# Conditioning matmuls of the second layer, moved from the first MLP to three stage changes

## The chip, the cores and the metric

The kernel runs on one core of a Trainium2 chip. The metric is the device time of one execution in microseconds (us). The kernel before took 1434.49 us (median of 3 runs, 1434.38 to 1434.61). The profile is one further execution with the hardware profiler on.

In the profile PE is the matrix engine (TensorE), PEld its weight load, DVE is VectorE, ACT is ScalarE, POOL is GpSimd, SP is SyncE, which issues DMAs here. L119 is line 119 of the kernel's file.

## What is computed

One inference step of a two-layer decoder trunk with width 1024: 512 prompt tokens and 8 samples of 4 tokens, 544 columns in all. Each layer has a token mixer and a squared-ReLU MLP, and every sub-layer is wrapped in normalisation and in shift, scale and gate vectors that come from a conditioning vector.

```python
def ada_params(c, w, b):
    mod = jax.nn.silu(c) @ w + b
    return jnp.split(mod[:, None, :], 6, axis=-1)
...
    for layer in range(DEPTH):
        sh_m, sc_m, g_m, sh_f, sc_f, g_f = ada_params(c, ada_w[layer], ada_b[layer])
        hin = rmsnorm(x, norm_g[layer, 0]) * (1.0 + sc_m) + sh_m
        j = layer // N_MIXERS
        if layer % N_MIXERS == 0:
            mix, buf, hn = rglru_mixer(hin, ...)
        else:
            mix, v = chunk_sgu_mixer(hin, ...)
        x = x + g_m * rmsnorm(mix, norm_g[layer, 1])
        hf = rmsnorm(x, norm_g[layer, 2]) * (1.0 + sc_f) + sh_f
        f = jnp.square(jax.nn.relu(hf @ mlp_w_up[layer])) @ mlp_w_down[layer]
        x = x + g_f * rmsnorm(f, norm_g[layer, 3])
```

`ada_w` is 1024 x 6144 per layer (24 MB). Each of its six sections of 1024 columns makes one vector per sequence, nine sequences in all. Section 0 (shift) and 1 (scale) of layer 1 are first needed when the first MLP ends, section 2 (gate), 3 and 4 when the gating unit ends, section 5 when the second MLP ends.

## The kernel before

Everything runs with features on the partitions and tokens on the free axis; the 544 tokens are two halves of 272 columns. A large product is done as three matmuls on split operands (high x high, high x low, low x high), issued by `mm3` through `mm`; both end in line 119, 128 x 128 weights against 272 columns, so nearly all matmuls carry the line L119. The names say what they multiply: HH and HL are the split normalised input, hi and lo the split weights, hh and hl the split hidden activations of the MLP, yh and yl those of a mixer's output.

The program's order is written by a counter of large matmuls (`Clock`, one tick per `mm`). Side work is a generator; `yield 44` means that its next piece is issued 44 large matmuls later. A scheduler then sets each engine's final order within what the data allow, so what was issued together may be parted.

The stages follow each other: RG-LRU mixer, first MLP, gating unit, second MLP. Each ends in `final_proj`, which projects first half 0, then half 1 of the tokens. After each half a `Stat` sums squares (ACT and DVE) and takes the mean over the features by one matmul with `dmean` (L390). A `Chain` per half then scales, adds the residual (L662), takes a second `Stat` and writes HH (ACT, L452) and HL (DVE, L453) for the next stage. That next stage starts in `first_sweeps`, half 0 first, one k-tile of HH after the other. So half 1 of the old projection covers the chain of half 0, and the sweep over half 0 covers the chain of half 1.

The conditioning of layer 1 is made by `ada_gen`, added as a task of the first MLP: three blocks of 2048 columns, each in eight steps of one k-tile. A step is two loads of 512 KB from SP's queue into the weight pool and four matmuls (L609) with a stationary operand of 32 columns, `tile_position=(0, 32 * g)`, so that the four use four column groups of PE. After eight steps a block is copied, turned by four transposes (L620) and added to the bias (`ada_add`, L568). `every` is 85 ticks.

The gating unit's `vsmp` has two more users of the narrow mode: L1397, in fours, and L1403, one alone with 256 columns.

Of the kernel before, what the change touches and what calls it, by code (L numbers as in the profile page):

```python
# [12 lines left out]
ALU = mybir.AluOpType  # L13
PSUM = bass.MemoryType.PSUM

P = 128
# [64 lines left out]
def trunk_kernel(  # L81
# [511 lines left out]
    def ada_gen(jobs, every):  # L593
        def load(l, blk, k):
            ts_ = [wtile("ada") for _ in range(2)]
            for i in range(2):
                c = blk * 2048 + i * 1024
                nc.sync.dma_start(ts_[i], ada_w[l, k * P:(k + 1) * P, c:c + 1024])
            return ts_

        steps = [(l, b, k) for l, b in jobs for k in range(KD)]
        nxt = load(*steps[0])
        yield every
        for i, (l, blk, k) in enumerate(steps):
            ts_, nxt = nxt, load(*steps[i + 1]) if i + 1 < len(steps) else None
            if k == 0:
                ps = aux()
            for g in range(4):
                nc.tensor.matmul(  # L609
                    ps[32 * g:32 * g + 32, :], scT[:, k, :], ts_[g // 2][:, (g % 2) * 512:(g % 2) * 512 + 512],  # L610
                    start=(k == 0), stop=(k == KD - 1), tile_position=(0, 32 * g))
            if k < KD - 1:
                yield every
                continue
            raw = slot("adas")
            A.copy(raw[:, 0:512], ps)
            yield 12
            pt = aux()
            for q in range(4):
                nc.tensor.transpose(pt[:, q * P:(q + 1) * P], raw[:, q * P:(q + 1) * P], ident)  # L620
            ptv = pt.rearrange("p (q g s) -> p q g s", q=4, g=4)
            for g in range(4):
                c = blk * 2048 + g * 512
                ada_add(l, c // D, (c % D) // P, 4, ptv[:, :, g, 0:9])
            for idx in ((0,), (1,), (2, 3))[blk]:
                ada_derive(l, idx)
            yield every - 12

    class Chain:


# [55 lines left out]
    def first_sweeps(key, chains, evac):  # L687

        for h in range(2):
            for grp in ((0, 1, 2, 3), (4, 5)):  # L690
                lhs = [st.get(key(m // 2)).lhs(m % 2) for m in grp]
                ps = [acc() for _ in range(len(grp) // 2)]
                for k in range(KD):
                    chains[h].need(k)
                    for i in range(len(grp)):
                        for a in (0, 1):
                            mm(ps[i // 2][:, i % 2, 0:HW], lhs[i][k][a], HH[:, k, HS[h]], k + a == 0, False)
                for i, m in enumerate(grp):
                    for k in range(KD):
                        mm(ps[i // 2][:, i % 2, 0:HW], lhs[i][k][0], HL[:, k, HS[h]], False, k == KD - 1)  # L700
                    if i % 2:
                        for j in range(2):
                            evac(m - 1 + j, ps[i // 2][:, j, 0:HW], h)

    def mix_add(m, ps, first):
# [3 lines left out]
        else:  # L709
            V.tensor_tensor(mv, mv, ps[:, :, 0:HW], op=ALU.add)  # L710

    def final_proj(lhs, rhs, both, groups, l, idx, nxt):


        A.activation(warm, epsc, AF.Abs_reciprocal_sqrt)
        S = [Stat(), Stat(nxt is None)]
        rows = LastRows(AM[l][idx]) if nxt is None else None
        for m in both:
            ps = acc()
            mm3(ps, lhs(m), rhs, (0, 1))  # L720
            mix_add(m, ps, False)
            for h in range(2):
                S[h].add(MIX[:, m, HS[h]])
        if rows:
            rows.add(both)
        chains = []
        for h in range(2):
            for grp, parts in groups[h]:
                if rows and h == 1 and grp[-1] == KD - 1:
                    rows.residual()  # L730
                if rows and h == 1 and grp[-1] == KD - 1:
                    for j, m in enumerate(grp):
                        ps = acc()
                        mm3(ps, lhs(m), rhs, (1,), col=0)
                        V.tensor_tensor(MIX[:, m, HS[1]], MIX[:, m, HS[1]], ps[:, 0, 0:HW], op=ALU.add)
                        S[1].add(MIX[:, m, HS[1]])
                        rows.finish_tile(j)
                    break
                ps = [acc() for _ in range(len(grp) // 2)]
                for ks in parts:  # L740
                    for i, m in enumerate(grp):
                        mm3(ps[i // 2], lhs(m), rhs, (h,), ks=ks, col=i % 2)
                        if i % 2 and ks is parts[-1]:
                            mv = MIX[:, m - 1:m + 1, HS[h]]
                            V.tensor_tensor(mv, mv, ps[i // 2][:, :, 0:HW], op=ALU.add)
                            S[h].add2(mv, slot("sq")[:, 0:T].rearrange("p (j n) -> p j n", j=2))
                            if rows and h == 1:
                                rows.add((m - 1, m))
            if rows and h == 1:
                rows.finish(S[1])  # L750
            else:
                chains.append(Chain(l, idx, S[h], h, nxt))
        return chains
# [475 lines left out]
    def state_out():  # L1229
        for (src, n, outs) in ((HST, 9, ((0, 1, h_prompt.rearrange("l s d -> (l s) d")),  # L1230
                                         (1, 9, h_sample.rearrange("l s d -> (l s) d")))),
                               (CST, 27, ((0, 3, conv_prompt.rearrange("l s j d -> (l s j) d")),
                                          (3, 27, conv_sample.rearrange("l s j d -> (l s j) d"))))):
            for b in range(3):
                pt = aux()
                for q in range(4):
                    nc.tensor.transpose(pt[0:n, q * P:(q + 1) * P], src[:, 4 * b + q, :], ident)
                o = slot("st")
                V.tensor_copy(o[0:n, 0:512], pt[0:n, :])
                for lo_, hi_, dst in outs:  # L1240
                    nc.gpsimd.dma_start(dst[:, b * 512:(b + 1) * 512], o[lo_:hi_, 0:512])
                yield 30
# [8 lines left out]
    def mlp(l, nxt, chains, tasks):  # L1251
        for q in range(4):
            hh, hl = [None] * 8, [None] * 8

            def evac(m, ps, h=None):
                if hh[m] is None:
                    hl[m] = slot("hl", F32R)
                    hh[m] = slot("hh", F32R)
                w = slot("hf")
                if h is None:  # L1260
                    dl, dh, dw = [t_[:, 0:T].rearrange("p (h n) -> p h n", h=2) for t_ in (hl[m], hh[m], w)]
                else:
                    dl, dh, dw = hl[m][:, HS[h]], hh[m][:, HS[h]], w[:, HS[h]]
                A.activation(dw, ps, AF.Relu)  # L1264
                A.activation(dw, dw, AF.Square)
                A.copy(dh, dw)  # L1266
                V.tensor_tensor(dl, dw, f32(dh), op=ALU.subtract)  # L1267

            if q == 0:
                first_sweeps(lambda c: ("u", l, 0, c), chains, evac)  # L1270
                for t in tasks:
                    clk.add(t)
            for c in range(3 if q == 0 else 0, 4):
                u = st.get(("u", l, q, c))
                for j in range(2):
                    ps = acc()
                    mm3(ps, u.lhs(j), hin_rhs, (0, 1))
                    evac(2 * c + j, ps[:, :, 0:HW])
            rhs = list(zip(hh, hl))
            if q == 3:  # L1280
                return final_proj(lambda m: st.get(("d", l, 3, m // 2)).lhs(m % 2), rhs, (0, 1),
                                  (singles(range(2, 8), 8),) * 2, l, 3, nxt)
            for c in range(4):
                u = st.get(("d", l, q, c))
                for j in range(2):
                    ps = acc()
                    mm3(ps, u.lhs(j), rhs, (0, 1))
                    mix_add(2 * c + j, ps, q == 0)
# [79 lines left out]
    def spatial_gate(chains):  # L1368
# [40 lines left out]
            V.bn_stats(stat[0:NSMP, 4, c, :], v)  # L1409

        first_sweeps(lambda c: ("su", c), chains, u_evac)
        t_prep = clk.add(sg_prepare(), 10)
        vts = []
        for c in range(6):
# [139 lines left out]
                nc.sync.dma_start(y_prompt[0, c0:c1, b * 512:(b + 1) * 512], o[0:n, 0:512])  # L1554
                yield 6

    chains = mlp(0, (1, 0), chains, [ada_gen([(1, 0), (1, 1), (1, 2)], 85), state_out()])
    chains = spatial_gate(chains)
    chains = mlp(1, None, chains, [])
    clk.drain(*[t for t in clk.tasks])  # L1560
# [30 lines left out]
```

## Time and profile before

| | |
|---|---|
| median of 3 runs | 1434.49 us |
| the profiled execution | 1435.27 us |
| its span on the core | 1433.5 us |
| PE busy | 1395.7 us (97%) |
| VectorE, ScalarE, GpSimd busy | 703.7, 632.5, 41.1 us |
| chain that ended last | PE 65%, of it L119 58% and L609 3%; issue 26% |
| mean granted clock of PE | 0.989 |
| bytes moved | 165.71 MB, 116 GB/s mean |

The span runs from the first to the last instruction. Busy time of PE is modelled, since matmuls overlap each other. A wait in a timeline stands in brackets, with what ended it. The chain of waits is followed back from the last instruction; "issue" in it is time in which the engine waited for nothing that the profile shows. A matmul on 32-bit operands that are not split is two instructions on PE, so a step of four L609 matmuls reads x8.

### The profile page before, as it was taken

How to read it: one execution, taken by the hardware profiler on the slowest of the kernel's cores; microseconds unless marked ns; L12 is line 12 of the kernel's file. 1: busy time of each engine (PE TensorE's matmuls, PEld its weight loads, DVE VectorE, ACT ScalarE, POOL GpSimd, SP SyncE). 2: the span in 40 equal slices, each digit the busy share in tenths (PEclk: the TensorE clock that was granted, in tenths of full speed). 3: DMA queues.
4: the chain of work that ended last, by engine and by line, in shares of the span. 5: the costliest groups of instructions: out<-in, count | busy, mean ns of one | idle time of the engine just before them, and what ended most of it. 6: DMA issues, size and time to landing. Idle time of an engine off the chain costs nothing.

```text
span 1433.5 us, 27033 instructions
## 1 busy us (share of the span) xinstructions
PE 1395.7 (97%) x11472; PEld 1319.4 (92%) x11472; DVE 703.7 (49%) x1442; ACT 632.5 (44%) x1160; POOL 41.1 (3%) x76
## 2 busy tenths in 40 slices
PE   8999999998999999999998999999899999999997
PEld 6899989997999999999997989999899999999996
DVE  4767476779422332333349446653972233333334
ACT  4465746846523413414425434432573341432523
POOL 1200000000100000000000200000000000000000
PEclk8999999999999999999999999999999999999998
DMA  9554554321545545543221333122232222222201
GB/s 309 174 173 130 163 151 149 103 89 60 180 154 174 170 157 173 170 157 115 62 86 60 95 96 107 61 74 62 90 100 91 89 89 89 89 89 89 89 1 63
DMA packets 132227, 165.71 MB, mean 116 GB/s; under 512 B 10168, under 2 KB 111560, under 8 KB 132106
## 3 DMA queue, kind: packets, MB, share of 16 engines
q1 hardware_dynamic: 130346, 161.89, 35.9%
q0 software_dynamic: 1760, 2.09, 0.7%
q8 instruction: 90, 1.47, 0.4%
q14 instruction: 31, 0.25, 0.1%
HBM read 161.31 MB, written 2.65 MB: 114 GB/s over the span
## 4 chain that ended last, share of the span: by engine, by line
PE 65%; issue 26%; DVE 5%; ACT 2%; DMA 1%; POOL 0%; SPq 0%; POOLq 0%; ACTq 0%; DVEq 0%
PE acc L119 58%; PE aux L609 3%; DVE lo L182 1%; PE acc L1478 1%; DVE MIX L448 1%; DVE X L662 1%; DMA xsr<-in_x_sample_dram 1%; DVE HL L453 1%; PE aux L1397 0%; PE aux L580 0%; DVE MIX L660 0%; PE aux L390 0%; ACT HH L452 0%; DVE rs L414 0%; DVE R L415 0%
## 5 line engine op out<-in xcount | busy, mean ns | idle before, releaser
L119 PE MATMUL acc<-HH,hi 128*128 128x272 f32 x1776 | 399.2, 293 | 12.6 <-ACT HH L452 11.2
L119 PE MATMUL acc<-HH,lo 128*128 128x272 f32 x1776 | 394.0, 292 | 3.4 <-DVE lo L182 3.4
L182 DVE TENSOR_TENSOR lo<-raw,hi 128x512 fp32r<-128x512 f32 (+1 forms) x404 | 263.2, 682 | 254.3 <-ACT hi L181 188.1
L119 PE MATMUL acc<-HL,hi 128*128 128x272 f32 x1776 | 355.4, 289 | 3.5 <-DVE HL L453 3.1
L181 ACT CAST hi<-raw 128x512 fp32r<-128x512 f32 (+1 forms) x404 | 230.3, 613 | 281.7 <-PE acc L119 159.2
L119 PEld LDWEIGHTS acc<-HH,hi 128*128 128x128 f32 x1776 | 293.6, 191 | 23.2 <-ACT HH L452 13.7
L119 PEld LDWEIGHTS acc<-HH,lo 128*128 128x128 f32 x1776 | 293.1, 191 | 11.5 <-issue 6.7
L119 PEld LDWEIGHTS acc<-HL,hi 128*128 128x128 f32 x1776 | 273.5, 189 | 10.9 <-issue 5.4
L119 PE MATMUL acc<-hh,lo 128*128 128x272 f32 x1024 | 230.0, 290 | 0.0
L119 PE MATMUL acc<-hh,hi 128*128 128x272 f32 x1024 | 229.8, 290 | 0.0
L119 PE MATMUL acc<-hl,hi 128*128 128x272 f32 x1024 | 229.7, 290 | 0.0
L119 PEld LDWEIGHTS acc<-hh,hi 128*128 128x128 f32 x1024 | 168.0, 188 | 3.9 <-issue 3.8
L119 PEld LDWEIGHTS acc<-hh,lo 128*128 128x128 f32 x1024 | 168.1, 188 | 3.7 <-issue 3.6
L119 PEld LDWEIGHTS acc<-hl,hi 128*128 128x128 f32 x1024 | 168.1, 188 | 3.6 <-issue 3.5
L1267 DVE TENSOR_TENSOR hl<-hf,hh 128x544 fp32r<-128x544 f32 (+1 forms) x76 | 47.7, 634 | 175.2 <-ACT hh L1266 175.0
L1264 ACT ACTIVATE hf<-acc 128x544 f32<-128x544 f32 (+1 forms) x76 | 41.2, 550 | 128.1 <-PE acc L119 126.1
L710 DVE TENSOR_TENSOR MIX<-MIX,acc 128x544 f32<-128x544 f32 x44 | 31.6, 717 | 75.9 <-PE acc L119 75.9
L119 PE MATMUL acc<-hi,HH 128*128 128x256 f32 x192 | 54.8, 285 | 0.0
L119 PE MATMUL acc<-hi,HL 128*128 128x256 f32 x192 | 54.6, 284 | 0.0
L119 PE MATMUL acc<-lo,HH 128*128 128x256 f32 x192 | 53.8, 280 | 0.0
L119 PE MATMUL acc<-yh,hi 128*128 128x272 f32 x208 | 52.7, 291 | 0.3 <-ACT MIX L708 0.3
L119 PE MATMUL acc<-yh,lo 128*128 128x272 f32 x208 | 52.6, 291 | 0.0
(332 smaller groups left out, 1444.5 us busy)
## 6 DMA issues: line engine op xcount, KB each, us to landing
ada<-in_ada_w_dram SPq DMA_DIRECT2D x96, 512.0 KB, 4.9
raw<-in_mlp_w_up_dram SPq DMA_DIRECT2D x64, 512.0 KB, 4.3
raw<-in_mlp_w_down_dram SPq DMA_DIRECT2D x64, 512.0 KB, 4.5
raw<-in_lru_w_in_dram SPq DMA_DIRECT2D x24, 512.0 KB, 4.5
raw<-in_sg_w_in_dram SPq DMA_DIRECT2D x24, 512.0 KB, 4.6
raw<-in_sg_w_out_dram SPq DMA_DIRECT2D x12, 512.0 KB, 4.2
raw<-in_lru_w_out_dram SPq DMA_DIRECT2D x8, 384.0 KB, 3.0
raw<-in_lru_w_out_dram SPq DMA_DIRECT2D x6, 512.0 KB, 6.4
```

Source lines behind the costliest of these rows:

```text
L119: nc.tensor.matmul(out, lhsT, rhs, start=start, stop=stop)
L181: A.copy(h_, raw[:, c:c + st])
L182: V.tensor_tensor(l_, raw[:, c:c + st], f32(h_), op=ALU.subtract)
L448: V.scalar_tensor_tensor(wv, X[:, k, c0:c1], Am[:, k, 0:1], R[:, c0:c1], op0=ALU.mult, op1=ALU.mult)
L453: V.scalar_tensor_tensor(HL[:, k, c0:c1], wv, sh[:, k, 0:1], f32(HH[:, k, c0:c1]), op0=ALU.add, op1=ALU.subtract)
L609: nc.tensor.matmul(ps[32 * g:32 * g + 32, :], scT[:, k, :], ts_[g // 2][:, (g % 2) * 512:(g % 2) * 512 + 512], start=(k == 0), stop=(k == ...
L662: V.scalar_tensor_tensor(X[:, j, c0:c1], MIX[:, j, c0:c1], Gm[:, j, 0:1], X[:, j, c0:c1], op0=ALU.mult, op1=ALU.add)
L710: V.tensor_tensor(mv, mv, ps[:, :, 0:HW], op=ALU.add)
L1264: A.activation(dw, ps, AF.Relu)
L1267: V.tensor_tensor(dl, dw, f32(dh), op=ALU.subtract)
L1478: nc.tensor.matmul(ps[p0:p0 + 32, 0, ck * P:(ck + 1) * P], vp[ck // 2, c][:, o:o + 32], wT[g], start=True, stop=True, tile_position=(0, p0))
```

## The change

A second generator, `ada_fill`, makes the same vectors from 512-column pieces: per step four loads of 256 KB from POOL's queue into four buffers of the general pool, 44 ticks later the four matmuls (L643), at the end one copy, four transposes (L650) and the adds. It is started by `final_proj` where half 1 begins, at three stage changes: sections 0 and 1 between RG-LRU and first MLP (eight steps), 2 and 3 between first MLP and gating unit (eight steps), 5 between gating unit and second MLP (four steps of two k-tiles). Section 4 stays in the first MLP, in four steps. `ada_gen` is no longer used for layer 1.

```diff
+    def ada_fill(l, c0, n, wait=44):
+        kk = 4096 // n // 2
+        nb = n // 512
+        for k0 in range(0, KD, kk):
+            ts_ = [slot("adf") for _ in range(4)]
+            for g in range(4):
+                k, c = k0 + g // nb, c0 + (g % nb) * 512
+                nc.gpsimd.dma_start(ts_[g][:, 0:512], ada_w[l, k * P:(k + 1) * P, c:c + 512])
+            yield wait
+            if k0 == 0:
+                ps = aux()
+            for g in range(4):
+                nc.tensor.matmul(ps[32 * g:32 * g + 32, :], scT[:, k0 + g // nb, :], ts_[g][:, 0:512],
+                                 start=(k0 == 0), stop=(k0 + kk == KD), tile_position=(0, 32 * g))
+        raw = slot("adas")
+        A.copy(raw[:, 0:512], ps)
+        yield 12
+        pt = aux()
+        for q in range(4):
+            nc.tensor.transpose(pt[:, q * P:(q + 1) * P], raw[:, q * P:(q + 1) * P], ident)
...
+    fills = {}
+    FILL = {(0, 1): (1, 0, 2048), (0, 3): (1, 2048, 2048), (1, 1): (1, 5 * D, 1024)}
...
         for h in range(2):
+            if h == 1 and (l, idx) in FILL:
+                fills[l, idx] = clk.add(ada_fill(*FILL[l, idx]))
...
                 first_sweeps(lambda c: ("u", l, 0, c), chains, evac)
+                clk.drain(fills[l, 1])
...
         first_sweeps(lambda c: ("su", c), chains, u_evac)
+        clk.drain(fills[0, 3])
...
-    chains = mlp(0, (1, 0), chains, [ada_gen([(1, 0), (1, 1), (1, 2)], 85), state_out()])
+    chains = mlp(0, (1, 0), chains, [ada_fill(1, 4 * D, 1024), state_out()])
```

What this makes of PE's order is seen at three places. At the end of the RG-LRU projection over half 1, PE's rows before are these; acc is the projection's sum, aux a small bank, pt the summed squares:

```order
L390 MATMUL aux_3849<-pt_3834,dmean 128x272
L119 MATMUL acc_3937<-yh_3401,lo_3533 128x272
L119 MATMUL acc_3937<-yh_3416,hi_3545 128x272
L119 MATMUL acc_3937<-yl_3415,hi_3545 128x272
L119 MATMUL acc_3937<-yh_3416,lo_3546 128x272
L119 MATMUL acc_3937<-HH,hi_3545 128x272
L119 MATMUL acc_3937<-HL,hi_3545 128x272
```

and with the change these (adf is a loaded piece of `ada_w`, scT the conditioning vectors):

```order
L390 MATMUL aux_3870<-pt_3842,dmean 128x272
L643 MATMUL aux_3845<-adf_3850,scT 32x512
L643 MATMUL aux_3845<-adf_3851,scT 32x512
L119 MATMUL acc_3970<-HH,hi_3588 128x272
L119 MATMUL acc_3970<-HL,hi_3588 128x272
L119 MATMUL acc_3970<-HH,lo_3589 128x272
L119 MATMUL acc_3970<-yh_3388,hi_3532 128x272
L119 MATMUL acc_3970<-yl_3387,hi_3532 128x272
L643 MATMUL aux_3845<-adf_3852,scT 32x512
L119 MATMUL acc_3970<-yh_3388,lo_3533 128x272
```

The second step of the first fill, four matmuls issued together, stands as a pair, then one alone five large matmuls later; the fourth follows after six more. Counted over the whole program, stretches of L643 with nothing else between number 21, 21 and 11 at the three stage changes; of these 53, 5 hold four matmuls, 12 two and 36 one.

In the first MLP a step stood whole before (ada is the loaded weight tile):

```order
L119 MATMUL acc_6234<-HH,hi_6186 128x272 x2
L119 MATMUL acc_6234<-HL,hi_6186 128x272 x2
L609 MATMUL aux_5588<-ada_6158,scT 32x512 x2
L609 MATMUL aux_5588<-ada_6159,scT 32x512 x2
L119 MATMUL acc_6234<-HH,lo_6187 128x272 x2
L119 MATMUL acc_6234<-HH,hi_6186 128x272 x2
```

and at the same count of large matmuls the change has only these:

```order
L119 MATMUL acc_6275<-HH,lo_6191 128x272 x2
L119 MATMUL acc_6275<-HH,hi_6227 128x272 x2
L119 MATMUL acc_6275<-HL,hi_6227 128x272 x2
L119 MATMUL acc_6275<-HH,lo_6228 128x272 x2
L119 MATMUL acc_6275<-HH,hi_6227 128x272 x2
L119 MATMUL acc_6275<-HL,hi_6227 128x272 x2
```

Nothing stands between the large matmuls there; the four steps that stay in this MLP are its first, each four L643 in a row.

On POOL, between the last work of the RG-LRU (graw, the gate weights) and the stores of the state (st) there stood before:

```order
L209 MEMSET graw_2839 128x896
L209 MEMSET graw_2925 128x896
L1241 DMA out_dram<-st_4492 16x1x32
L1241 DMA out_dram<-st_4492 8x512
L1241 DMA out_dram<-st_4539 16x1x32
```

and now, ahead of the same stores, all loads of the first fill and some of the MLP's; the first of them are:

```order
L209 MEMSET graw_2925 128x896
L638 DMA adf_3756<-in_ada_w_dram 128x512
L638 DMA adf_3757<-in_ada_w_dram 128x512
L638 DMA adf_3758<-in_ada_w_dram 128x512
L638 DMA adf_3759<-in_ada_w_dram 128x512
L638 DMA adf_3850<-in_ada_w_dram 128x512
L638 DMA adf_3851<-in_ada_w_dram 128x512
```

SP's queue loses the loads of layer 1 from `ada_w`, and POOL's gains 96 of half their size.

## Rows read from the trace of the kernel before

**Rows 1.** The page, part 1: engine, busy us, share, instructions.

```profile
PE 1395.7 (97%) x11472; PEld 1319.4 (92%) x11472; DVE 703.7 (49%) x1442; ACT 632.5 (44%) x1160; POOL 41.1 (3%) x76
```

**Rows 2.** Stretches A, B, C: length, busy PE, PEld, DVE, ACT, POOL; PEclk, DMA, GB/s.

```profile
310.00:375.00 65.00, 58.40 (x432) 56.68 (x431) 56.72 (x123) 40.37 (x91) 1.78 (x4) 0.95 0.30 94
738.00:800.00 62.00, 56.44 (x428) 53.63 (x427) 51.22 (x112) 34.80 (x69) 6.43 (x12) 1.00 0.27 80
995.00:1062.00 67.00, 59.03 (x426) 57.03 (x426) 58.34 (x126) 41.76 (x91) 2.50 (x5) 0.95 0.27 83
sum 194.00, PE 173.87 PEld 167.35 DVE 166.27 ACT 116.93 POOL 10.71; mean PE 57.96 PEld 55.78 DVE 55.42 ACT 38.98 POOL 3.57
```

**Rows 3.** Timeline of PE in A: start us, us, instruction, wait before.

```profile
327.66 0.59 PE L119 MATMUL acc<-HH,hi 128*128 128x272 f32 x1 [3.02 <-ACT HH L452]
...
333.27 0.34 PE L119 MATMUL acc<-HH,hi 128*128 128x272 f32 x1
...
353.90 0.39 PE L119 MATMUL acc<-HH,hi 128*128 128x272 f32 x1 [0.92 <-ACT HH L452]
...
355.88 0.39 PE L119 MATMUL acc<-HH,hi 128*128 128x272 f32 x1 [0.71 <-ACT HH L452]
```

**Rows 4.** Timeline of PE in C.

```profile
1015.76 0.40 PE L119 MATMUL acc<-HH,hi 128*128 128x272 f32 x1 [3.01 <-ACT HH L452]
...
1019.36 0.33 PE L119 MATMUL acc<-HH,hi 128*128 128x272 f32 x1
...
1041.75 0.40 PE L119 MATMUL acc<-HH,hi 128*128 128x272 f32 x1 [1.79 <-ACT HH L452]
...
1043.73 0.59 PE L119 MATMUL acc<-HH,hi 128*128 128x272 f32 x1 [0.72 <-ACT HH L452]
...
1046.61 0.36 PE L119 MATMUL acc<-HH,hi 128*128 128x272 f32 x1
```

**Rows 5.** Chain of waits in the first MLP: start us, us, what.

```profile
564.17 1.00 PE aux L609 x8
...
576.40 1.00 PE aux L609 x8
...
659.59 0.99 PE aux L609 x8
...
662.73 75.90 PE acc L119 x607
```

**Rows 6.** Chain of waits in the RG-LRU.

```profile
203.09 1.83 PE aux L609 x10
...
217.49 0.99 PE aux L609 x6
```

**Rows 7.** Timeline of PE in the gating unit, a narrow matmul alone.

```profile
824.87 0.28 PE L119 MATMUL acc<-hi,HH 128*128 128x256 f32 x1
824.99 0.28 PE L119 MATMUL acc<-lo,HH 128*128 128x256 f32 x1
825.19 0.62 PE L1403 MATMUL aux<-vw,sel 128*32 128x256 f32 x2
...
826.08 0.28 PE L119 MATMUL acc<-lo,HH 128*128 128x256 f32 x1
```

**Rows 8.** Timeline of PE in B.

```profile
781.90 1.05 PE L1397 MATMUL aux<-raw,HSM 128*32 128x256 f32 x10 [0.66 <-DVE HSM L444]
```

**Rows 9.** Timeline of POOL in C.

```profile
1023.02 0.52 POOL L1463 DMA_DIRECT2D lg<-in_sg_ln_g_dram  x1 [160.80 <-DVE HL L453]
1026.06 0.51 POOL L1464 DMA_DIRECT2D lb<-in_sg_ln_b_dram  x1 [2.51 <-ACT HH L452]
```

**Rows 10.** DMA issues: what, queue, KB each, median us to landing.

```profile
raw<-in_mlp_w_up_dram SPq DMA_DIRECT2D x64, 512.0 KB, 4.3
...
bin<-in_sg_b_in_dram POOLq DMA_DIRECT2D x6, 128.0 KB, 3.7
```

**Rows 11.** Stretch of 10 us in C, columns as in rows 2.

```profile
1020.00:1030.00 10.00, 9.69 (x76) 9.40 (x74) 10.00 (x24) 5.31 (x11) 1.02 (x2) 1.00 0.54 168
```

More of the change, by code (lines that the diff above doesn't have):

```diff
@@ L627, in ada_gen @@
             yield every - 12
+    def ada_fill(l, c0, n, wait=44):
[18 more added lines that the diff above has]
+            nc.tensor.transpose(pt[:, q * P:(q + 1) * P], raw[:, q * P:(q + 1) * P], ident)
+        ptv = pt.rearrange("p (q g s) -> p q g s", q=4, g=4)
+        for g in range(4):
+            c = c0 + (g % nb) * 512
+            sec, kt = c // D, (c % D) // P
+            if g < nb:
+                ada_add(l, sec, kt, 4, ptv[:, :, g, 0:9])
+            else:
+                m_ = MOD[l][:, sec, kt:kt + 4, :]
+                V.tensor_tensor(m_, m_, ptv[:, :, g, 0:9], op=ALU.add)
+        for sec in range(c0 // D, (c0 + n) // D):
+            if sec in (1, 2, 4, 5):
+                ada_derive(l, (1, 2, 4, 5).index(sec))
     class Chain:
```

## The prediction, made before the changed kernel was run

> **What bounds the kernel now.** The page comes first: the matrix engine (PE) is busy for 1395.7 us of a span of 1433.5 [rows 1], so time is won only by giving PE less to do or by filling its 37.8 us of idle time. The second view is the table of stretches, cut at the three places where one projection ends and the next begins: A (310 to 375 us, RG-LRU to first MLP), B (738 to 800, first MLP to gating unit), C (995 to 1062, gating unit to second MLP). There PE is busy for 173.87 of 194.00 us, so 20.1 of the 37.8 us of idle time lie in these places: 6.6, 5.6 and 8.0 [rows 2]. The timeline of PE shows what a long wait costs beyond itself. In A PE stands for 3.02 us until the first HH tile is ready, and the next 24 matmuls start 5.61 us apart in all instead of 3.0 (24 at 0.125, the pitch of the clean stretch 75.90 / 607 [rows 5]): the granted clock of A is 0.95, that of B 1.00 [rows 2, 3]. In C the waits of 3.01 us and of 1.79 and 0.72 us are followed by 16 and 12 slow matmuls, 1.6 and 1.4 us lost [rows 4]. Idle and slow time that other work could take: 20.1 + 2.6 + 1.6 + 1.4 = 25.7 us.
>
> **What is removed.** The chain of waits runs through PE in the first MLP. Seven conditioning steps there lie from 576.40 to 659.59, so one period is 11.88 us; its 85 large matmuls are worth 85 x 0.125 = 10.63, so a step of four L609 matmuls, 32 columns wide each, costs 1.256 us, not only the 1.00 us of its row, because the matmuls around it start later too. The period that also holds the four transposes (564.17 to 576.40) is 0.35 longer [rows 5]. 20 of 24 steps and two of three sets of transposes go: 20 x 1.256 + 2 x 0.35 = 25.8 us, all on the path, since PE has no wait in this MLP. Their loads go from SP's queue too, which frees nothing that PE waited for.
>
> **What is added.** The same 80 matmuls come back at A, B and C, but no longer as 20 sets of four. The order of PE shows them cut apart by large matmuls: a pair, a single, a single. In A the eight steps make 21 separate stretches, in B 21, in C (four steps) 11: 53 stretches, of which 5 hold four matmuls, 12 two and 36 one. The four that stay in the MLP are whole. So the term to size is the price of a stretch, not of a matmul.
>
> The trace before has stretches of other lengths. Three L609 matmuls take 0.99 us, as long as four; five take 1.83, so a fifth that finds no free column group costs 0.83 more [rows 6]. Lengths of one to four therefore cost about the same. For one alone between large matmuls the nearest row is L1403, 32 columns wide, 256 columns of data instead of 512: from the large matmul before it to the third after it are 1.09 us where three pitches of 0.12 make 0.36, so it costs 0.73 [rows 7]. Half of 0.83 is its data, 0.42; going in and out costs 0.31. With 512 columns: 0.83 + 0.31 = 1.15. Bounds: 0.83 if going in and out is free, 1.26 if a single costs what a whole step does. I take 1.15, from the row that is nearest in kind: 53 x 1.15 = 61.0, and three sets of transposes at 0.35: 62.0 us. With the bounds 45.0 and 67.8.
>
> The Trainium skill (TensorEngine Tiling (Array Packing), Theoretical Speedup) gives up to 4x where the stationary side is at most 32 wide. Taken per matmul it would make each of the 80 cost a quarter of a step, 0.31, and the added work equal to the removed; the row of the lone L1403, 0.73 instead of about 0.2, says that the gain belongs to matmuls that stand together (Key Properties on the same page: changing the tiling mode drains the engine).
>
> **What the waits take off.** A stretch in front of a wait costs nothing as long as the wait lasts. In A five stretches (5.8 us) now stand ahead of the sweep that waited 3.02 us: the wait goes, and with it the slow 2.6 us. B and C likewise. But the second half's normalisation starts from the end of the same projection, four to six stretches later, and its mean over the features is a matmul (L390) that stands in PE's queue behind more of them. So it comes later with PE, and the waits at the start of the second half stay: 0.92 and 0.71 in A [rows 3], 0.66 in B [rows 8], 1.79 and 0.72 with the slow 1.4 in C [rows 4], together 6.2. Taken off: 25.7 - 6.2 = 19.5 us. Bounds: all 25.7, or as little as 12 if the chains are late by what PE is.
>
> **Loads.** Each step now issues four DMAs of 256 KB from POOL, which was idle there. No row shows such a load. POOL needs 0.52 us per issue [rows 9], so 2.1 for four; landing lies between 3.7 us (128 KB from POOL) and 4.3 (512 KB from SP) [rows 10]: about 6 to 6.5 us per step. From one step to the next lie 44 large matmuls, 5.5 us, and three stretches, 3.5: 9 us. The first steps' buffers are free before the stage begins, the later ones' when the step before has been multiplied. I take no wait, cost 0, with 2.5 us to spare; below zero it can't go, since no wait on a load ended here before. VectorE and ScalarE do the same small adds as before, elsewhere, 0.2 us each beside PE. The state outputs now queue on POOL between such loads; only the stores' own landing hangs on that.
>
> **Sum.** -25.8 + 62.0 - 19.5 = +16.7 us. The profiled execution took 1435.27 us (span 1433.5 and 1.8 around it), 0.8 above the median of 1434.49; the sum goes on the median: 1451 us.
>
> **Rivals.**
> (1) The other side, faster: going in and out of the narrow mode hides under the neighbours' weight loads, so that a stretch costs its data alone, 0.83, and everything idle is taken: 45.0 - 25.8 - 25.7 = -6.5, 1428 us. It decides from a price below (25.8 + 19.5 - 1.05) / 53 = 0.84 per stretch; with 0.83 to 0.9 the time lies within 0.2%. For it: the fifth matmul of [rows 6]. Against it: that one followed its own kind, and the lone L1403 paid 0.31 more. Chance 0.09, and 0.07 for the band about no change.
> (2) Loads come late: matmuls stand in PE's queue in order, and a single that waits for its 256 KB holds the large ones behind it. If landing on POOL's queue is 3.5 us longer than taken, each step waits about 1 us: 20 more, 1471 us, and waits as long as in [rows 3] would bring slow matmuls again. For it: one queue, issues in order, no row of this size. Against it: the 2.5 us of margin, and at A, B and C the transfer engines are 0.27 to 0.30 busy [rows 2]. Chance 0.12.
> The Trainium skill (SBUF — State Buffer, The "DVE blocks DMA" trap) says that VectorE copies in a two-port mode lock GpSimd out while it writes descriptors, an issue of about 620 ns becoming about 3100; by that, as an estimate, four issues take 12 us, 3 more than the 9 there are, and 20 steps lose 60. The trace does not agree for this place: beside a VectorE busy for 10.00 of 10 us [rows 11] POOL's issues at 1023 and 1026 us took 0.52 and 0.51 [rows 9], and the page names copies and tensor_scalar for it, not the two-input operations that run here.
> (3) The change does what it seems to: the 20 steps vanish in the waits. That would need them to stay whole: 20 x 1.256 + 1.05 - 25.8 - 19.5 = -19, 1415 us. The order of PE excludes the whole steps; nothing but a quarter price per matmul would bring it. It is within the 0.09 of (1), at most 0.02.
>
> **Numbers.** Forecast 0.72 (1451; its own range 1440 to 1460, price 1.0 to 1.26 and 12 to 25 taken), (2) 0.12, (1) 0.09, no change 0.07. Slower by more than 0.2% (2.9 us, about what this kernel's measurement tells from nothing): 0.72 + 0.12 = 0.84; within: 0.07; faster: 0.09. The range holds the forecast and part of (2) and leaves out (1): 1440 to 1466.
>
> **What would show it.** In the profile after: PE's busy time higher by some 30 us; no L609 of layer 1 in the first MLP but four whole steps, the stage shorter by about 26; at A and B no wait of 3 us and clock 1.00, yet each some 14 to 20 us longer, C about 5; a row of one L643 matmul between large ones that costs 1.1 to 1.2. Wrong if singles cost under 0.9 us, if PE waits on DMA in adf rows for more than a few us, or if A and B grow by less than 8 us each.

## The result

The changed kernel takes 1453.2 us (median of 4 runs, 1452.6 to 1453.8), the kernel before 1434.4 beside it; the ratio is 1.0131 (95% interval 1.0113 to 1.0148). That is 18.8 us slower; +16.7 and 1451 were forecast, with a range of 1440 to 1466.

The page of the changed kernel, part 1, as in [rows 1]:

```profile
PE 1426.9 (98%) x11476; PEld 1321.4 (91%) x11476; DVE 705.8 (49%) x1446; ACT 632.8 (44%) x1161; POOL 94.1 (6%) x172
```

PE executes four instructions more than before, yet it is busy for 31.2 us longer. The groups of PE's instructions, kept apart by shape (count, busy time, mean ns of one), show where:

```profile
L643 PE MATMUL aux<-adf,scT 128*32 128x512 f32 x192 | 59.8, 605 | 0.0
L609 PE MATMUL aux<-ada,scT 128*32 128x512 f32 x128 | 17.9, 604 | 0.0
```

Each matmul of the form leaves two records: 96 matmuls of the fill (L643) fill 59.8 us, 64 matmuls of the old form (L609, all of layer 0) fill 17.9. One matmul takes 0.62 us of busy time in the first group and 0.28 in the second, where four stand together and share the time of one. PE's timeline of the changed kernel shows, one after the other, a single in place A, a wait that was not there before, and a whole step in the first MLP.

```profile
324.52 0.29 PE L119 MATMUL acc<-yl,hi 128*128 128x272 f32 x1
324.73 1.04 PE L643 MATMUL aux<-adf,scT 128*32 128x512 f32 x2
325.71 0.39 PE L119 MATMUL acc<-yh,lo 128*128 128x272 f32 x1
325.94 0.28 PE L119 MATMUL acc<-yh,hi 128*128 128x272 f32 x1
326.06 0.29 PE L119 MATMUL acc<-yl,hi 128*128 128x272 f32 x1
...
359.79 1.06 PE L643 MATMUL aux<-adf,scT 128*32 128x512 f32 x8
363.57 0.50 PE L119 MATMUL acc<-HH,hi 128*128 128x272 f32 x1 [2.72 <-ACT hf L1304]
363.88 0.43 PE L119 MATMUL acc<-HH,lo 128*128 128x272 f32 x1
364.10 0.43 PE L119 MATMUL acc<-HH,hi 128*128 128x272 f32 x1
...
397.75 0.29 PE L119 MATMUL acc<-HL,hi 128*128 128x272 f32 x1
397.97 1.06 PE L643 MATMUL aux<-adf,scT 128*32 128x512 f32 x8
398.97 0.39 PE L119 MATMUL acc<-HL,hi 128*128 128x272 f32 x1
399.20 0.41 PE L119 MATMUL acc<-HH,lo 128*128 128x272 f32 x2
399.44 0.42 PE L119 MATMUL acc<-HH,hi 128*128 128x272 f32 x2
```

What a stretch costs is read from the starts of the large matmuls around it, not from its own row, which overlaps them. A pitch is the time from one large matmul's start to the next where nothing disturbs them, 0.125 us. Single: from 324.52 to the third large matmul behind it at 326.06 are 1.54 us; three pitches of 0.125 would be 0.375, so it pushed the rest back by 1.17. Whole step: 397.75 to the fourth at 399.44 are 1.69, less 0.50 is 1.19. The pairs that stand between large matmuls alone read 1.17 to 1.19. One matmul, two or four cost nearly the same.

At C the waits went as far as the chain of the first half goes, and not beyond. What PE waited for there in the changed kernel (total us, times, longest):

```profile
PE acc L119 <- ACT HH L452: 2.5, 2, 1.8
PE acc L119 <- DVE lo L182: 1.0, 1, 1.0
PE acc L119 <- DVE HL L453: 0.3, 1, 0.3
```

The 3.01 us of [rows 4] are gone; the 1.79 and 0.71 at the start of the second half stand. At A and B the second half's waits are others than before: at A 0.44 us is left of 0.92 and 0.71, and the 2.72 above are new; at B the 0.66 are gone, and 0.94 (on ScalarE's ug, L1422) are new. The table of stretches, columns as in [rows 2], with the ends moved to where the same work now ends:

```profile
310.00:394.00 84.00, 80.84 (x496) 59.38 (x495) 58.88 (x130) 42.41 (x96) 12.24 (x23) 0.98 0.44 139
733.00:812.00 79.00, 78.06 (x483) 56.62 (x482) 51.41 (x117) 34.54 (x68) 20.97 (x38) 1.00 0.46 150
1008.00:1082.00 74.00, 70.19 (x461) 57.80 (x461) 59.13 (x131) 42.22 (x93) 6.77 (x13) 0.98 0.33 104
```

PE idles for 3.2, 0.9 and 3.8 us there, 7.9 in place of 20.1 us.

### The profile page after: what moved, and what is told of

It is laid out like the page before. It is cut to its first block, busy times and chain, and to the rows that moved or that the text cites. A ratio compares the mean times of both kernels' runs of the same rounds, so it can differ in the third digit from the quotient of the medians.

```text
span 1452.0 us, 27213 instructions
## 1 busy us (share of the span) xinstructions
PE 1426.9 (98%) x11476; PEld 1321.4 (91%) x11476; DVE 705.8 (49%) x1446; ACT 632.8 (44%) x1161; POOL 94.1 (6%) x172
## 4 chain that ended last, share of the span: by engine, by line
PE 69%; issue 27%; ACT 2%; DVE 1%; DMA 1%; POOL 0%; SPq 0%; POOLq 0%; ACTq 0%; DVEq 0%
PE acc L119 60%; PE aux L643 4%; PE aux L609 1%; PE acc L1520 1%; DMA xsr<-in_x_sample_dram 1%; PE aux L580 0%; PE aux L1438 0%; PE aux L390 0%; PE aux L531 0%; ACT HH L452 0%; PE aux L1444 0%; PE aux L1402 0%; DVE lo L182 0%; PE aux L966 0%; PE aux L1277 0%
## 5 line engine op out<-in xcount | busy, mean ns | idle before, releaser
L119 PE MATMUL acc<-HH,hi 128*128 128x272 f32 x1776 | 398.0, 293 | 8.1 <-ACT HH L452 2.9
L119 PE MATMUL acc<-HH,lo 128*128 128x272 f32 x1776 | 393.6, 291 | 1.3 <-DVE lo L182 1.3
L119 PE MATMUL acc<-HL,hi 128*128 128x272 f32 x1776 | 355.9, 289 | 0.6 <-DVE HL L435 0.3
L119 PEld LDWEIGHTS acc<-HH,hi 128*128 128x128 f32 x1776 | 291.4, 190 | 33.2 <-issue 17.2
L119 PEld LDWEIGHTS acc<-HH,lo 128*128 128x128 f32 x1776 | 291.3, 190 | 16.5 <-issue 14.3
L119 PEld LDWEIGHTS acc<-HL,hi 128*128 128x128 f32 x1776 | 273.5, 188 | 10.6 <-issue 5.4
L119 PE MATMUL acc<-hh,hi 128*128 128x272 f32 x1024 | 229.7, 290 | 0.0
L119 PE MATMUL acc<-hl,hi 128*128 128x272 f32 x1024 | 229.0, 289 | 0.0
L119 PE MATMUL acc<-hh,lo 128*128 128x272 f32 x1024 | 228.8, 289 | 0.0
L119 PEld LDWEIGHTS acc<-hh,hi 128*128 128x128 f32 x1024 | 167.9, 188 | 4.7 <-issue 4.6
L119 PEld LDWEIGHTS acc<-hl,hi 128*128 128x128 f32 x1024 | 168.0, 188 | 1.9 <-issue 1.9
L119 PEld LDWEIGHTS acc<-hh,lo 128*128 128x128 f32 x1024 | 168.0, 188 | 1.1 <-issue 1.0
L1304 ACT ACTIVATE hf<-acc 128x544 f32<-128x544 f32 (+1 forms) x76 | 41.3, 552 | 116.2 <-PE acc L119 113.8
L638 POOL DMA_DIRECT2D adf<-in_ada_w_dram x96 | 51.5, 539 | 613.0 <-PE acc L119 283.0
L643 PE MATMUL aux<-adf,scT 128*32 128x512 f32 x192 | 59.8, 605 | 0.0
L119 PE MATMUL acc<-hi,HH 128*128 128x256 f32 x192 | 54.7, 285 | 0.0
L119 PE MATMUL acc<-hi,HL 128*128 128x256 f32 x192 | 54.5, 284 | 0.0
L119 PE MATMUL acc<-lo,HH 128*128 128x256 f32 x192 | 53.8, 280 | 0.0
```

The lines of the kernel that those rows point to most:

```text
L119: nc.tensor.matmul(out, lhsT, rhs, start=start, stop=stop)
L638: nc.gpsimd.dma_start(ts_[g][:, 0:512], ada_w[l, k * P:(k + 1) * P, c:c + 512])
L643: nc.tensor.matmul(ps[32 * g:32 * g + 32, :], scT[:, k0 + g // nb, :], ts_[g][:, 0:512], start=(k0 == 0), stop=(k0 + kk == KD), tile_posit ...
```

## Experiments

The theory: a stretch costs PE about 1.17 us whether it holds one, two or four of a step's matmuls, 0.83 for its 512 columns of data and some 0.34 for going into the narrow form and out; so the loss comes from the scheduler cutting 20 steps into 53 stretches. The rivals: (1) the price goes by matmul; (2) the place costs, since work at a stage change delays the next stage's chain; (3) POOL's loads cost. Further rivals have letters or numbers in the text that was written ahead of each run.

**one_ahead.** The loads go out a step earlier, so that more of a step is there when its turn comes.

```diff
+        nxt = load(0)
         for k0 in range(0, KD, kk):
-            ts_ = [slot("adf") for _ in range(4)]
+            ts_, nxt = nxt, load(k0 + kk) if k0 + kk < KD else None
...
             yield wait
```

> The four loads of each moved step are issued one step earlier, so that fewer steps are cut: 32 stretches stand at A, B and C where the changed kernel has 53; four whole steps stay in the first MLP in both. Theory (each stretch costs 1.17 us, the displacement read in the trace after, however many of the four matmuls it holds): 21 stretches less x 1.17 = -24.6, if the waits are used as much as before (some 18 us): 1453.2 - 24.6 = 1428.6; up to 1434 if bigger stretches find fewer waits. Rival 1 (the price goes by matmul, not by stretch: 80 moved matmuls in both): 1453 +- 1.5. Rival 2 (what costs is that the work stands at the stage changes, where it delays the chain of the next stage): 1450 to 1453. Rival 3 (POOL's loads late): also faster, since the loads come earlier, but then with DMA waits in the changed kernel, of which its trace shows none.

1429.8 us (1429.4 to 1430.4), ratio 0.9966 (0.9953 to 0.9979). 21 stretches fewer, 23.4 us less than the changed kernel, 1.1 each; the same 80 matmuls stand at the same three stage changes. Price by matmul and price of the place fall. An earlier load alone would also fit rival 3, if the changed kernel waited on loads; no wait of its PE at A, B or C ends on a DMA.

**wide_tiles.** Two loads of 1024 columns per step into the weight pool, two steps ahead.

```diff
-                nc.gpsimd.dma_start(ts_[g][:, 0:512], ada_w[l, k * P:(k + 1) * P, c:c + 512])
+                nc.gpsimd.dma_start(ts_[i], ada_w[l, k * P:(k + 1) * P, c:c + 1024])
...
+        ahead = [load(k0) for k0 in ks[:2]]
...
```

> The moved steps load two tiles of 1024 columns in place of four of 512, two steps ahead, on the same queue. 22 stretches at A, B and C (most steps whole, three times two steps or nearly two in one stretch) where the changed kernel has 53. Theory (price by stretch, 1.17 us for up to four matmuls; 0.83 more for a second step in the same stretch): 53 x 1.17 = 62.0 becomes 22 x 1.17 + 3 x 0.83 = 28.2, so -33.8 if the waits are used as before: 1419; if whole steps use no wait at all (some 18 us back): 1437. Rival 1 (price by matmul): 1453 +- 1.5, since the 80 matmuls are the same. Rival 2 (position at the stage changes): above 1445.

1424.6 us (1421.7 to 1426.6), ratio 0.9927 (0.9912 to 0.9942): within the theory's range and faster than the kernel before. PE's page row and its timeline:

```profile
PE 1396.8 (98%) x11476; PEld 1317.8 (92%) x11476; DVE 706.2 (50%) x1446; ACT 632.5 (44%) x1161; POOL 66.9 (5%) x124
```

```profile
323.68 0.29 PE L119 MATMUL acc<-yh,hi 128*128 128x272 f32 x1
323.90 1.06 PE L652 MATMUL aux<-ada,scT 128*32 128x512 f32 x8
324.89 0.40 PE L119 MATMUL acc<-yl,hi 128*128 128x272 f32 x1
...
344.43 0.29 PE L119 MATMUL acc<-HH,hi 128*128 128x272 f32 x1
344.65 1.92 PE L652 MATMUL aux<-ada,scT 128*32 128x512 f32 x14
346.50 1.77 PE L119 MATMUL acc<-HL,hi 128*128 128x272 f32 x12
```

The same count of instructions (x11476) keeps PE busy for 30.1 us less than in the changed kernel. Seven matmuls in one stretch push the next large one to 2.07 us behind the last, four to 1.21: the second step adds 0.86, its data alone.

**sp_queue.** The changed kernel's loads from SP's queue.

```diff
-                nc.gpsimd.dma_start(ts_[g][:, 0:512], ...)
+                nc.sync.dma_start(ts_[g][:, 0:512], ...)
```

> The loads of the moved steps go out on SP's queue in place of POOL's; nothing else. The steps are cut nearly as before: 50 stretches at A, B and C where the changed kernel has 53. Theory (price by stretch): 3 x 1.17 = -3.5, so 1449.7 +- 2. Rival 3 (POOL's queue, its descriptors or its port is what costs): below 1440.

1449.1 us (1447.8 to 1449.8), ratio 1.0098 (1.0083 to 1.0113): 4.1 us less than the changed kernel. Three stretches fewer make 3.5 of it; POOL's queue is not what costs.

**cut_in_place.** The kernel before, nothing moved, each step of the first MLP in four pieces.

```diff
             for g in range(4):
+                if l == 1 and g:
+                    yield 8
                 nc.tensor.matmul(
...
-                yield every
+                yield every - 24 * l
...
```

> The kernel before, with each of the 24 steps in the first MLP cut into four single matmuls, eight sum matmuls apart; nothing is moved, no load is changed. 24 stretches of four become 96 of one. Theory (price by stretch): 24 steps of 1.19 become 96 x 1.17: 112.3 - 28.6 = +83.8, so 1518. Rival 1 (price by matmul: a quarter step costs a quarter of 1.19): 1434 +- 2. Rival 4 (a single costs its data alone, 0.83, because nothing else is paid away from the stage changes): 96 x 0.83 - 28.6 = +51, so 1485. Rival 2 (the price is that of the stage changes): 1434 to 1440.

1516.7 us (1515.9 to 1517.6), ratio 1.0572 (1.0554 to 1.0589). Its timeline:

```profile
399.32 0.29 PE L119 MATMUL acc<-hl,hi 128*128 128x272 f32 x1
399.54 1.04 PE L611 MATMUL aux<-ada,scT 128*32 128x512 f32 x2
400.51 0.40 PE L119 MATMUL acc<-hl,hi 128*128 128x272 f32 x1
400.75 0.42 PE L119 MATMUL acc<-hh,lo 128*128 128x272 f32 x2
401.00 0.42 PE L119 MATMUL acc<-hh,hi 128*128 128x272 f32 x2
```

399.32 to 401.00 less four pitches: 1.18 for a single, in the middle of an MLP; all 96 singles of this run read 1.17 to 1.18. Cutting alone, with no new place and no new load, costs 82 us. This is the price by itself, and it settles rivals 1, 2 and 4.

**thin.** Most moved matmuls on 64 columns of data instead of 512; the sums of the other columns are left out.

```diff
+                w = 512 if k0 in (0, KD - kk) else 64
-                nc.tensor.matmul(ps[32 * g:32 * g + 32, :], ..., ts_[g][:, 0:512],
+                nc.tensor.matmul(ps[32 * g:32 * g + 32, 0:w], ..., ts_[g][:, 0:w],
```

> The changed kernel with the matmuls of all moved steps but the first and the last of each fill cut from 512 columns to 64 (that part of the second layer's conditioning sums is left out, so the output differs); loads, waits and queue are unchanged. At A, B and C 47 stretches of 64 columns and 11 of 512 stand where the changed kernel has 53 of 512. It splits the 1.17 us of a stretch. Theory (0.83 for the data of 512 columns, 0.34 for going into the narrow mode and out again): a thin stretch displaces 0.34 + 0.83 x 64/512 = 0.44 us; 47 x 0.44 + 11 x 1.17 = 33.6 in place of 62.0, two thin steps in the first MLP -1.5: 1423, and up to 1433 if short stretches use less of the waits. Rival D (all 1.17 is the entering and leaving, the data costs nothing): 1.17 a stretch, 1453 + 6 = 1459. Rival E (all of it goes with the columns): 0.15 a stretch, about 1409.

1429.4 us (1429.0 to 1429.8), ratio 0.9966 (0.9952 to 0.9979), within the theory's 1423 to 1433. The price is clearer in its timeline than in its time:

```profile
322.37 0.29 PE L119 MATMUL acc<-yl,hi 128*128 128x272 f32 x1
322.59 0.30 PE L644 MATMUL aux<-adf,scT 128*32 128x64 f32 x2
322.82 0.39 PE L119 MATMUL acc<-yh,lo 128*128 128x272 f32 x1
323.05 0.29 PE L119 MATMUL acc<-yh,hi 128*128 128x272 f32 x1
323.17 0.29 PE L119 MATMUL acc<-yl,hi 128*128 128x272 f32 x1
```

322.37 to 323.17 less three pitches is 0.43; 0.44 was expected. Less 0.10 of data, 0.33 is paid whatever the columns are.

**full_width.** The cut steps of the first MLP as matmuls of full width.

```diff
...
+                if l == 1:
+                    nc.tensor.matmul(ps, ident, w_, start=(k + g == 0), stop=(k + g == KD + 2))
+                    continue
...
```

> The kernel with the steps of the first MLP cut in place into four singles, with each single as a matmul of 128 columns of weights by the same 512 columns of data in fp32, not of 32 columns at a tile position (its sums are others, so the output differs). Theory (the 0.34 belongs to the narrow form): 96 singles at their data alone, as L390 with 272 columns displaces 0.45 to 0.47 where nothing else stands beside it, which is 0.85 for 512: 96 x 0.85 - 24 x 1.19 = +53, so 1488. Rival F (any matmul of another kind between the float32r ones pays it): 1.17 to 1.19 each, 1517 as with the narrow singles.

1488.0 us (1487.1 to 1488.6), ratio 1.0374 (1.036 to 1.0388). In its timeline a single costs 398.94 to 400.30 less four pitches, 0.86 (all 96 read 0.85 to 0.87):

```profile
398.94 0.28 PE L119 MATMUL acc<-hl,hi 128*128 128x272 f32 x1
399.06 1.02 PE L613 MATMUL aux<-ada,ident 128*128 128x512 f32 x2
399.52 0.69 PE L119 MATMUL acc<-hl,hi 128*128 128x272 f32 x1
400.05 0.41 PE L119 MATMUL acc<-hh,lo 128*128 128x272 f32 x2
400.30 0.42 PE L119 MATMUL acc<-hh,hi 128*128 128x272 f32 x2
```

So 0.32 of the 1.17 belongs to the narrow form. The large matmuls' operands are of type float32r and those of the conditioning matmuls, narrow or full, of type fp32; that change, which both kinds make, costs nothing that shows here. The run widens the operand and drops `tile_position` in one edit, so by itself it does not say which of the two pays; but L1403 [rows 7] is 32 columns wide and is given no `tile_position` in the program, and it pays its 0.31 too.

**pairs_of_steps and fours_of_steps.** The wide tiles, with two or four steps issued at once.

```diff
+            if j % 2 == 0:
+                ts_s, ahead = ahead, []
+                for k1 in ks[j + 2:j + 4]:
+                    ahead.append(load(k1))
+                yield 2 * wait
...
```

This is the edit of the pairs; the fours have `j % 4` and `ks[j + 4:j + 8]`.

> The wide tiles, and two steps issued together with one wait of 44 x 2 between (eight matmuls in one stretch where the scheduler leaves them together): 16 stretches at A, B and C and 2 in the first MLP, where the wide tiles alone have 22 and 4. Theory (price by stretch: 0.34 for the stretch and 0.83 for each step in it): 8 stretches less x 0.34 = -2.7 against the wide tiles: 1422 +- 3, the waits used deciding the rest. Rival 1 (price by matmul): 1424.6. Rival 3 (tiles held longer, weights late): above 1427, with waits of the L119 matmuls on DMA.

> As the pairs, but four steps issued together: 7 stretches at A, B and C and 1 in the first MLP. Up to 16 of the 16 weight tiles are asked for by one fill at a time. Theory (price by stretch): 18 stretches less than the wide tiles x 0.34 = -6.1: 1418.5 +- 4, if the three-us waits still take as much. Rival 3 (weight tiles held, weights late): above 1425, with waits of the L119 matmuls on DMA; or the four steps stand ahead of the waits and not in them: the rows of the three-us waits come back, up to +10.

Pairs: 1423.8 us (1422.7 to 1424.9), ratio 0.9924 (0.991 to 0.9937). That is in the expected range, but can't be told from the wide tiles, so whether 8 stretches fewer brought their 2.7 us stays open. Fours: 1428.8 us (1427.4 to 1430.6), ratio 0.9963 (0.995 to 0.9975); the forecast missed by 6 beyond its range's upper end. What PE waited for in the fours, of it one line for A, one for B and two for C:

```profile
PE aux L654 <- DMA ada<-in_ada_w_dram: 3.6, 7, 0.8
...
PE aux L654 <- DMA ada<-in_ada_w_dram: 3.5, 3, 2.0
...
PE acc L119 <- DVE lo L182: 3.6, 4, 2.3
PE acc L119 <- ACT HH L452: 3.0, 2, 2.3
```

With eight loads asked for at once the fill's matmuls wait for 7.1 us, the rival's cost, though it falls on them and not on the large ones as written. The rival's other half came too: at C the large matmuls wait for 6.6 us, up to 2.3 at a time.

**left_out.** The changed kernel without the 20 moved steps.

```diff
+        if c0 != 4 * D:
+            yield wait
+            for sec in range(c0 // D, (c0 + n) // D):
+                V.memset(MOD[l][:, sec], 0.5)
...
```

> The changed kernel without the moved steps: the 20 steps that went to A, B and C are left out, loads and matmuls, and their sections are set to a constant (so the output differs); the four steps that stay in the first MLP are kept. It is the floor under both kernels and measures two terms of the sum apart. Theory (removed steps -25.8 by the prediction, -24.5 by the 1.19 that a whole step displaces): 1434.4 - 25.8 = 1408.6, or 1410. Then the added stretches cost the changed kernel 1453.2 - 1408.6 = 44.6 net, which leaves 62.0 + 1.05 - 44.6 = 18.4 for the waits they filled, as the sum of the three stages gives it (17.8). Rival G (the added stretches fill hardly any wait, and the price is lower, some 0.85): the floor is the same 1408.6, but the waits of three us stand in its trace less by no more than 5 than in the changed kernel's. Rival H (the steps in the first MLP cost more than their displacement): below 1400.

1410.8 us (1409.7 to 1412.3), ratio 0.9833 (0.982 to 0.9846): 24.0 us under the kernel before that was run beside it. This time is called the floor below. Its waits in A:

```profile
PE acc L119 <- ACT HH L452: 4.7, 3, 3.0
PE aux L390 <- DVE pt L384: 1.8, 1, 1.8
PE acc L119 <- DVE HL L453: 1.1, 1, 1.1
PE acc L119 <- DVE lo L182: 1.0, 1, 1.0
```

8.6 us, where the changed kernel has 3.1; B has 5.6 against 0.9, C 7.9 against 3.8. So 14.3 us of idle time were filled, and rival G (a lower price, and hardly any wait filled) falls. With the floor every kernel can be split: stretches x 1.17 + 1.05 (three sets of transposes), and 0.83 for each double stretch, less what it lies above 1410.8, is what the waits took. That last column is a remainder and not a reading.

| kernel | stretches at A, B, C | added work, us | above the floor | taken by the waits |
|---|---|---|---|---|
| changed | 53 | 63.1 | 42.4 | 20.7 |
| sp_queue | 50 | 59.5 | 38.3 | 21.2 |
| one_ahead | 32 | 38.5 | 19.0 | 19.5 |
| wide_tiles (three double) | 22 | 29.3 | 13.8 | 15.5 |

By this the cut steps take some 5 us more off the waits than whole ones do, and pay 34 us for it. It is not idle time: PE idles for 8.4 us at A, B and C with the wide tiles and for 7.9 with the cut steps. What the 5 us are is not shown.

**wide_tiles_64.** The wide tiles with 64 ticks between steps.

```diff
-    def ada_fill(l, c0, n, wait=44):
+    def ada_fill(l, c0, n, wait=64):
```

> The wide tiles with 64 ticks between steps in place of 44: the first step of each place comes after the half's last projection, nearer to the three-us waits. 24 stretches at A, B and C where the wide tiles have 22. Theory (price by stretch, waits used as with the wide tiles): 1424.6 + 2 x 0.34 = 1425 +- 2. If steps that stand nearer to the waits fill more of them (up to 4 us of the 6 us left at C): 1420 to 1422. If they come so late that the next stage's first matmuls wait for the conditioning: above 1428.

1424.2 us (1423.3 to 1426.4), ratio 0.9929 (0.9915 to 0.9942): the theory's first case; nothing more was won. The wide tiles, the pairs and this one are the fastest versions, all about 0.7% under the kernel before.

## Why the prediction came right

*Removed, -25.8.* The floor shows -24.0, so the term was 1.8 too large. Of this 1.2 is the price: a period of the chain [rows 5] gave 1.256 a step, while a step pushes the large matmuls back by 1.19 to 1.20. The period holds something else of about 0.06, which no row shown names. The rest is no price, since the waits of A differ too in left_out:

```profile
327.56 0.40 PE L119 MATMUL acc<-HH,hi 128*128 128x272 f32 x1 [3.02 <-ACT HH L452]
327.79 0.29 PE L119 MATMUL acc<-HH,lo 128*128 128x272 f32 x1
...
333.80 0.73 PE L390 MATMUL aux<-pt,dmean 128*128 128x272 f32 x2 [1.84 <-DVE pt L384]
```

The wait of 3.02 us is that of [rows 3], but no slow matmuls follow it here: from 327 to 333 us the granted clock is 1.00 (2.4 GHz), where the kernel before has 0.50 (1.2 GHz). PE then reaches the sum over the features (L390) sooner and waits there for 1.84 us. So the slow 2.6 us in A, which the prediction counted beside the idle time, do not always come with the wait (after the same 3 us they are absent in full_width too, and present in cut_in_place), and where they are absent PE waits for 1.84 us of that time at the L390.

*Added, +62.0.* This is the term on which the sign rests, and it came from one row of another kind, the lone L1403 [rows 7]. Measured are 1.17 a stretch against 1.15, so +63.1 with the transposes. The split was right too: 0.83 and 0.31 taken, 0.83 to 0.86 and 0.32 to 0.33 found. Both bounds are excluded, 0.83 by the singles, and 1.26 even for a whole step.

*Taken by the waits, -19.5.* By the floor it is 20.7. That is what is left when the other terms are taken off, so that the terms then add up to the measured time (63.1 - 20.7 - 24.0 = +18.4, the medians say +18.8) proves nothing; 14.3 of the 20.7 are seen as idle time that is gone, and the other 6.4 are not read row by row. By places the agreement is looser. From the first L390 of one stage change to that of the next (after C: to that at the end of the second MLP), in us:

| | before | changed | left_out |
|---|---|---|---|
| with A | 430.8 | 425.5 | 406.7 |
| with B | 257.3 | 275.1 | 257.3 |
| with C | 401.5 | 408.4 | 401.4 |

Against the kernel before, the stage with A is 5.2 us shorter, that with B 17.8 longer, that with C 6.9 longer. With 24.0 removed, A grew by 18.8. The waits then took 24.9 - 18.8 = 6.1 in A, 24.9 - 17.8 = 7.1 in B and 13.2 - 6.9 = 6.3 in C, where 7.6, 4.9 and 7.1 had been counted. That the total came so near is in part luck: the errors of -1.5, +2.2 and -0.8 cancel.

A is short because of a step that the prediction does not have. At the second half's sweep PE waited 2.72 us for ScalarE (hf, L1304), which empties the first half's sums; the next large matmuls started 0.22 to 0.23 us apart (363.88, 364.10). So the granted clock of A is 0.98 and not the 1.00 forecast. The same wait stands with 2.7 in one_ahead and sp_queue and is absent with the wide tiles. ScalarE's order goes with it. In the kernel before, and with the wide tiles, ScalarE empties two sums before it writes the second half's first HH; in the three kernels with the wait it writes HH first, and that stood waiting for VectorE. ScalarE before, and then in the changed kernel:

```profile
350.50 0.38 ACT L1264 ACTIVATE hf<-acc 128x272 f32<-128x272 f32 x1
...
360.18 0.49 ACT L452 ACTIVATE HH<-MIX,MOD 128x240 fp32r<-128x240 f32 x1 [1.82 <-DVE MIX L448]
```

Why the order differs was not tried. B took 2.2 more than counted, and 1.5 more than its idle time of [rows 2]. The price is not lower there: B's singles that stand between large matmuls alone read 1.17 to 1.18, as elsewhere. The starts name two parts of it. L1397 stood in seven stretches before (the ten records of [rows 8] and six more 26 us later, where the changed kernel has sixteen in one) and stands in six now, 0.8 less; and four waits of L119 held the next start back by 0.16 more than their idle time each, 0.6 together. With the 4.6 us of idle time that is gone (5.6 less the new 0.94) that makes 6.1 of the 7.1; 1 us stays open. C went as forecast: the 1.79 and 0.72 of its second half stayed.

*Loads, 0.* Right: no wait of PE at A, B or C ends on the loads. A 256 KB load from POOL landed in 3.9 us, by the list of DMA issues of the changed kernel; 3.7 to 4.3 had been taken.

```profile
adf<-in_ada_w_dram POOLq DMA_DIRECT2D x96, 256.0 KB, 3.9
```

*The rivals.* (1) needed a price below 0.84; only a full-width matmul has about that, 0.86. (2) did not occur here, but did with eight loads at once. (3) was put at 0.02 since the steps are cut, and that is the right reason. Its 1415 for whole steps was too low, as the wide tiles show: 22 stretches at 1424.6. Its -19.5 for the waits doesn't hold for whole steps, which took 15.5.

## What to carry to other kernels

Narrow matmuls that share the array are to be priced by the stretch in which they stand, not one by one: when work is moved, count the stretches in the final order of the engine before and after. What split them here hung on the loads, four per step; fewer and earlier loads kept most steps whole and turned a loss of 1.3% into a gain of 0.7%. By which rule the scheduler parts them, no run shows. Filling waits is worth no more than the waits: 20 us here, with 24 taken out elsewhere.

## What was not expected of the hardware

A narrow fp32 matmul alone (32 columns wide) between float32r matmuls pays 0.32 to 0.33 us beside its data, with 64 columns of data (0.43 in all) as with 512 (1.17); a full-width fp32 one between the same neighbours pays nothing that shows (0.86 for 512 columns). And the row of a stretch hides this: 1.04 us of busy time stand for 1.17 of lost starts, 0.30 for 0.43.
